# A hybrid scan and Fourier layer: read-out and state copies moved to ScalarE, branch products spread, one division of PSUM

## The chip, the cores and the metric

The kernel runs on one core of a Trainium2 chip. The core has TensorE (PE: matmuls, with their weight loads as PEld), VectorE (DVE), ScalarE (ACT), GpSimd (POOL) and SyncE (SP, which here issues nearly all DMAs). Each engine works through its own queue in order; semaphores make one wait for another. The metric is the device time of one execution in microseconds, given as the median of several runs.

## The reference, cut to what matters

One layer of a diffusion backbone for 128 context and 1024 latent tokens (T = 1152 in all), width 1024:

```python
proj = h @ w_in                       # q, ff, fb, v, zA, u, zB, gA, gB
# branch A: gated linear recurrence, forward and backward, 8 heads, dk = dv = 128
S_t = diag(f_t) S_{t-1} + k_t v_t^T ;  o_t = S_t^T q_t
o = (o_f + o_b) * rsqrt(mean(o*o) + EPS) * gnorm_w
yA = o * silu(zA)
# branch B: real part of a 2-D DFT over positions and channels of u
yB = yF * silu(zB)
merged = sigmoid(gA) * (yA @ w_pa) + sigmoid(gB) * (yB @ w_pb)
out = merged @ w_o                    # then residual and final norm
```

The final states of the context tokens (both directions, every head) are an output as well (`new_state`).

## The kernel before, in words

All float32 products are made as three float32r products of a high and a low part (`mm3`: high by high, high by low, low by high). So each weight block is loaded, its high part is cast on ACT (`w_hi`, `wh`), and the low part is subtracted on POOL or DVE (`w_lo`, `wl`).

The stages in order of time are: normalisation and the first gate (to about 100 us); v for all heads (`project_v`, to about 164 us); the other columns of `w_in`, in pairs of 128 columns by a seven-product scheme (`pair`, to about 850 us, with the Fourier branch and the first scan levels interleaved); the scans with the branch products in between (about 850 to 1163 us); the last branch products and `w_o` to the end.

PSUM has eight banks. Up to the end of v they are divided into `d` (six banks, used in turn by the first gate and v) and `s` (two). Then that division is closed and another one is opened: `d` two, `s` two, `o` four. The pairs take `d`, `o`, `o` in turn (`any_ps`). A tile of the new division waits until the tile of the old one that lay on its bank has been read.

The scans are run by a loop over n = 0 to 9 (here: rounds). Round n walks a string of letters, `PATTERN[n]`, and each letter advances one generator by one step:

- **E** (`scan_blocks`, head n): five steps, E1 to E5, for the block sizes 4, 8, 16 (lines 781 to 792), 32 and 64. Each runs small matmuls over km, kk and qq into an `s` bank, and grows kk and qq by decay factors on DVE (L465, in place, 128x1152). The merges into a32 (L479) are on DVE, the copies into km (L472) and att (L803 to L816) on ACT.
- **L** (`scan_rest`, head n-1): transposes of kk (kt_ps, copied by ACT, L843), then the products kv and the state chain S on DVE (L856), then three groups of read-out matmuls into `o` banks. In the chain the first chunk of each direction gives the new state: `ns`, copied out of PSUM on DVE (L853) and stored by SP (L861). After each read-out group ACT squares and sums (L885) and takes the root (L887), and DVE takes the reciprocal (L869) and multiplies (L870, `scaled`).
- **Y** (the rest of `scan_rest`, head n-2): transpose of the scaled read-out, multiplication by the gate gz on DVE (L899), store to DRAM by SP (L908).
- **F** (`dense`): one half of a branch product. 12 matmuls go into a `d` bank, and DVE multiplies by the gate and so evacuates it: L936, or L938 followed by an add on POOL (L939). Each F loads its gate tile (gs) on SP, with three buffers; every second F loads a new weight block.
- **V** (`late_v`): the part of v that is left for here.

The order of matmuls on PE in the scans is that of the letters, forced by dependencies (`queued`). The order on the other engines is set by the scheduler's own timeline of the program. `ns` has no buffer of its own: it takes turns with the gz tiles in a ring of three (tag `gz`), and a gz slot is free when its store has landed.

Of the kernel before, what the change touches and what calls it, by code (L numbers as in the profile page):

```python
# [11 lines left out]
F32 = mybir.dt.float32  # L12
F32R = mybir.dt.float32r
I32 = mybir.dt.int32
AF = mybir.ActivationFunctionType
ALU = mybir.AluOpType
PSUM = bass.MemoryType.PSUM

P = 128
# [6 lines left out]
TW = 384  # L26
# [26 lines left out]
LATE = (4, 8, 16)  # L53
GRAN = 4
PIECES = ((0, 640), (640, T))
PATTERN = (['VEVVEVVEVVEVVE', 'VEVLVLEVVLVELVVLEVLFELFLF'] + 6 * ['EYLFYLEYLFELFFFEFLELFLF'] +
           ['YLFYLFYLFLFFFLFLFLF', 'YFYFYFFF'])
HW = T // 2
W0 = 1280
# [11 lines left out]
def diffusion_step(ctx: ExitStack, tc: tile.TileContext, xT, x_tok, w_pr, w_v, w_ada, w_ada_gt,  # L71
                   w_pab, w_o, state, vecs, b_gt, fnorm, pos_c, pos_row_t, pos_col_t, masks_i, mask_d, chan_dft, ctx_dft,
                   seq_dft, sign_row, y, new_state):
    nc = tc.nc

    def pool(name, bufs, **kw):
        return tc.tile_pool(name=name, bufs=bufs, reuse_waits="tile", **kw)
# [3 lines left out]
    banks = {}  # L81

    def open_psum(**bufs):
        stack = ExitStack()
        for tag, n in bufs.items():
            banks[tag] = stack.enter_context(pool("ps_" + tag, n, space=PSUM))
        return stack

    psum = open_psum(d=6, s=2)

    v_dr = dram.tile([NH, P, NCH, P], F32, name="v_dr")
    ya_dr = dram.tile([NH, P, T], F32, name="ya_dr")
# [19 lines left out]
        yield  # L112
        tc.cur_priority = p + 1

    def dense_ps():
        return banks["d"].tile([P, 512], F32, tag="d", name="d_ps")

    def scan_ps(tag="s"):
        return banks[tag].tile([P, 512], F32, tag=tag, name=tag + "_ps")

    ident = const.tile([P, P], F32, name="ident")
    make_identity(nc, ident)
# [92 lines left out]
    with pool("st", 1, side="right") as st, pool("st2", 2, side="right") as st2:  # L215
# [119 lines left out]
        e_ps = {}  # L335

        def gate0(k, a, b):

            for i in range(2):
                w_ = slice(i * P, (i + 1) * P)  # L340
                if k == 0:
                    e_ps[i, a] = dense_ps()[:, :b - a]
                ps = e_ps[i, a]
                mm3(ps, [(e_hi[:, k, w_], e_lo[:, k, w_], *h_at(k, a, b))], nc.tensor.matmul, k == 0, k == KT - 1)
                if k == KT - 1:
                    n = -(-(b - a) // SW)
                    w = (b - a) // n
                    for p in range(n):
                        go = va.tile([P, SW], F32, tag="vo", name="go", bufs=2)[:, :w]
                        nc.scalar.activation(go, ps[:, p * w:(p + 1) * w], AF.Sigmoid)  # L350
                        nc.sync.dma_start(g_dr[i, 0, :, a + p * w:a + (p + 1) * w], go)


        warm = dense_ps()
        e_raw = vb.tile([P, KT, 2 * P], F32, tag="wr", name="w_raw")
        e_hi, e_lo = (va.tile([P, KT, 2 * P], F32R, tag="w" + x, name="e_" + x) for x in "hl")
        was, abs_ = [], []
# [41 lines left out]
    def project_v(pr, chunks, p):  # L399
        raw = vb.tile([P, KT, 2 * P], F32, tag="wr", name="w_raw")  # L400
        nc.sync.dma_start(raw, w_v[pr])
        hi, lo = split_w(raw, KT, 2 * P, p)
        for c in chunks:
            ps = dense_ps()[:, :2 * P]
            mm3(ps, [(*h_at(k, c * P, (c + 1) * P), hi[:, k, :], lo[:, k, :]) for k in range(KT)])
            vo = va.tile([P, SW], F32, tag="vo", name="vo", bufs=2)[:, :2 * P].rearrange("p (h v) -> p h v", h=2)
            nc.vector.tensor_copy(vo, ps)
            nc.sync.dma_start(v_dr[2 * pr:2 * pr + 2, :, c, :].rearrange("h p v -> p h v"), vo)
# [8 lines left out]
    with pool("tg", 1, side="right") as tg:  # L417
        for nth, pr in enumerate((0, 2, 1, 3)):
            with tc.issue_after(last_ada[-1].ins):
                project_v(pr, range(5 if pr in LATE_V else 0, NCH), (vb, va)[nth % 2])  # L420
            for k in ((0,1,2,3), (), (), ())[pr]:
                for j in range(2):
                    js = slice(j * SW, (j + 1) * SW)
                    r = tg.tile([P, 2, 2, SW], F32, name="r")
                    for d in range(2):
                        for t, x in enumerate((h1, h2)):
                            hi, lo = x[k + 4 * d]
                            nc.gpsimd.tensor_tensor(out=r[:, d, t, :], in0=hi[:, js].bitcast(F32), in1=lo[:, js].bitcast(F32),
                                                    op=ALU.add)
# [5 lines left out]
                        nc.scalar.copy(hi[:, js], ts[:, w])  # L435
                        nc.vector.tensor_tensor(out=lo[:, js], in0=ts[:, w], in1=hi[:, js].bitcast(F32), op=ALU.subtract)
    ph1.close()
    psum.close()
    psum = open_psum(d=2, s=2, o=4)
    banks_in_turn = cycle("doo")  # L440

    def any_ps():
        return scan_ps(next(banks_in_turn))
# [380 lines left out]
    def scan_rest(hd):  # L824
        kk, qq, att, tot = heads.pop(hd)
        vt = s1.tile([P, T], F32, name="vt").rearrange("p (c v) -> p c v", v=P)
        nc.sync.dma_start(vt, v_dr[hd])
        S = s1.tile([P, 2, KT, P], F32, name="S")
        nc.sync.dma_start(S[:, 0, 0, :], state[0, hd])
        nc.sync.dma_start(S[:, 1, KT - 1, :], state[1, hd])  # L830


        ns = s2.tile([P, TW], F32, tag="gz", name="ns", bufs=3)[:, :2 * P].rearrange("p (d v) -> p d v", d=2)
        jobs = [(0, 0), (1, 0)]
        for j in range(KT - 1):
            jobs += [(0, 1 + j), (1, KT - j)]
        kts = []
        for b in range(0, len(jobs), 4):
            kt_ps = scan_ps("o")
            for n, (d, c) in enumerate(jobs[b:b + 4]):  # L840
                transpose(kt_ps[:, n * P:(n + 1) * P], in_=kk[:, d, c * P:(c + 1) * P], identity=ident)
            kts.append(s2.tile([P, HW], F32, name="kt_sb", bufs=4)[:, :4 * P].rearrange("p (c t) -> p c t", c=4))
            nc.scalar.copy(kts[-1], kt_ps)  # L843
            if b % 8:
                yield
        for b in range(0, len(jobs), 4):
            kv = scan_ps("o")
            for n, (d, c) in enumerate(jobs[b:b + 4]):
                matmul(kv[:, n * P:(n + 1) * P], lhsT=kts[b // 4][:, n, :], rhs=vt[:, c, :], start=True, stop=True)
            for n, (d, c) in enumerate(jobs[b:b + 4]):  # L850
                kvn = kv[:, n * P:(n + 1) * P]
                if c == 0:
                    nc.vector.tensor_copy(ns[:, d, :], kvn)  # L853
                else:
                    j = c - 1
                    nc.vector.scalar_tensor_tensor(out=S[:, d, j + (-1 if d else 1), :], in0=S[:, d, j, :],  # L856
                                                   scalar=tot[:, d, c:c + 1], in1=kvn, op0=ALU.mult, op1=ALU.add)
            if b % 8:
                yield
        for d in range(2):  # L860
            nc.sync.dma_start(new_state[hd, d], ns[:, d, :])  # L861


        ss = s1.tile([P, NCH], F32, name="ss", bufs=2)
        ons = []

        def scaled(g, ps, on):
            sg = ss[:, 3 * g:3 * g + 3]
            nc.vector.reciprocal(sg, sg)  # L869
            nc.vector.tensor_tensor(out=on, in0=ps[:, :TW].rearrange("p (c v) -> p c v", v=P),  # L870
                                    in1=sg.unsqueeze(2).broadcast_to([P, 3, P]), op=ALU.mult)
            ons.append(on)

        for g in range(3):
            ps = scan_ps("o")
            for c in range(3 * g, 3 * g + 3):
                oc = ps[:, (c - 3 * g) * P:(c - 3 * g + 1) * P]
                matmul(oc, lhsT=att[:, c, :], rhs=vt[:, c, :], start=True, stop=c == 0)
                if c:
                    for d in range(2):  # L880
                        matmul(oc, lhsT=qq[:, 1 - d, c * P:(c + 1) * P], rhs=S[:, d, c - 1, :], start=False, stop=d == 1)

            on = s2.tile([P, HW], F32, tag="kt_sb", name="on", bufs=4)[:, :TW].rearrange("p (c t) -> p c t", c=3)
            for c in range(3):
                nc.scalar.activation(on[:, c], ps[:, c * P:(c + 1) * P], AF.Square, accum_out=ss[:, 3 * g + c:3 * g + c + 1])  # L885
            sg = ss[:, 3 * g:3 * g + 3]
            nc.scalar.activation(sg, sg, AF.Sqrt, bias=eps, scale=1.0 / P)  # L887
            if g:
                scaled(g - 1, *last)
            last = ps, on  # L890
            yield
        scaled(2, *last)
        for g in range(3):
            gz = s2.tile([P, TW], F32, name="gz", bufs=3)
            nc.sync.dma_start(gz, gz_dr[hd, :, g * TW:(g + 1) * TW])
            yt = scan_ps("o")
            for c in range(3):
                transpose(yt[:, c * P:(c + 1) * P], in_=ons[g][:, c, :], identity=ident)
            nc.vector.tensor_tensor(out=gz, in0=yt[:, :TW], in1=gz, op=ALU.mult)  # L899
            if hd == NH - 1 and g < 2:  # L900

                if g == 0:
                    ys2.append(new_y(3, 0))
                a, b = g * TW, min((g + 1) * TW, HW)
                hi, lo = (x[:, a:b] for x in ys2[3])
                nc.scalar.copy(hi, gz[:, :b - a])
                nc.vector.tensor_tensor(out=lo, in0=gz[:, :b - a], in1=hi.bitcast(F32), op=ALU.subtract)
            nc.sync.dma_start(ya_dr[hd, :, g * TW:(g + 1) * TW], gz)  # L908
            yield
# [92 lines left out]
    for n in range(NH + 2):  # L1002
# [3 lines left out]
        done, rest = rest, scan_rest(n - 1) if 0 < n <= NH else iter(())  # L1006
        for what in PATTERN[n]:
            next({"E": blocks, "L": rest, "Y": done, "F": fill, "V": late}[what], None)
# [8 lines left out]
    op = ctx.enter_context(pool("op", 1))  # L1017
# [46 lines left out]
    for c in range(NCH):  # L1064
# [3 lines left out]
        for ks in [slice(k, k + 1) for k in range(KT)] if c == 0 else [slice(0, KT)]:  # L1068
            nc.scalar.copy(mh[:, ks, :], merged[:, ks, cs_])
            (nc.gpsimd if c else nc.vector).tensor_tensor(out=ml[:, ks, :], in0=merged[:, ks, cs_],  # L1070
                                                          in1=mh[:, ks, :].bitcast(F32), op=ALU.subtract)
# [17 lines left out]
        for n, (a, b) in enumerate(((0, 512), (512, 768), (768, D)) if last else ((0, 512), (512, D))):  # L1089
            ns_ = slice(a, b)  # L1090
            ps = any_ps()[:, :b - a]
# [115 lines left out]
```

## Time and profile before

| | before |
|---|---|
| median of 3 runs | 1323.48 us (1321.5 to 1328.47) |
| the profiled execution | 1325.72 us, span 1323.9 us |
| busy: PE / PEld | 1246.3 us (94%) / 1172.0 us (89%) |
| busy: DVE / ACT / POOL | 843.2 (64%) / 624.4 (47%) / 475.3 us (36%) |
| mean granted TensorE clock | 0.981 |

How to read the rows that follow: a row of the timeline has start and length in microseconds, engine, source line, operation, output <- input, shapes and count; in brackets stand the idle time of the engine before it and what ended that. A row of a view by windows has the stretch, its length, and for each engine its busy time in it. A row of waits has total, number and longest. PEclk is the granted TensorE clock (1.00 is full).

### The profile page before, as it was taken

Reading aid. Unit: us, or ns where it says so; the run is one execution under the profiler, and the core shown is the slowest. Engines: PE = TensorE matmul, PEld = TensorE weight load, DVE = VectorE, ACT = ScalarE, POOL = GpSimd, SP = SyncE. Lnnn points to the kernel's source line nnn. Section 1 sums busy time; section 2 is a strip of 40 time slices with the busy share of each in tenths; the row PEclk is TensorE's granted clock in tenths of the full one; section 3 lists DMA queues with packets and bytes.
Section 4 is the critical chain, followed back from the end, with each engine's and each line's share of the span. In section 5 each row is a group of like instructions: output and inputs, shape, how many; then the busy total and the mean of one; then the engine's idle time right before and its main releaser. Section 6 shows DMA issues by size and latency. Waiting matters only on the chain. (4 is left out here: it accounts for less than half of the span.)

```text
span 1323.9 us, 31278 instructions
## 1 busy us (share of the span) xinstructions
PE 1246.3 (94%) x12768; PEld 1172.0 (89%) x12768; DVE 843.2 (64%) x1391; ACT 624.4 (47%) x1290; POOL 475.3 (36%) x359
## 2 busy tenths in 40 slices
PE   4899999999999999999999999987988989999998
PEld 2679999999989999999999998987888879999886
DVE  7737743434357677677767645486878988475554
ACT  5542232454446655655655544454544545332332
POOL 4515523233412312222121216432232445565563
PEclk8899989999999999999999999998999999999999
DMA  8542233434444655555555663765666754676432
GB/s 313 220 172 60 76 109 118 135 101 148 146 153 163 209 179 165 201 184 161 204 186 163 213 227 106 251 229 165 225 210 220 241 176 131 186 241 198 141 121 96
DMA packets 126162, 229.88 MB, mean 174 GB/s; under 512 B 11441, under 2 KB 78786, under 8 KB 121794
## 3 DMA queue, kind: packets, MB, share of 16 engines
q1 hardware_dynamic: 125730, 226.83, 51.6%
q8 instruction: 100, 1.64, 0.5%
q10 hardware_dynamic: 288, 1.05, 0.3%
q14 instruction: 44, 0.36, 0.1%
HBM read 154.82 MB, written 73.02 MB: 172 GB/s over the span
## 5 line engine op out<-in xcount | busy, mean ns | idle before, releaser
L628 POOL TENSOR_TENSOR wl<-raw,wh 128x512 fp32r<-128x512 f32 x81 | 114.7, 1416 | 449.6 <-ACT wh L627 448.1
L627 ACT CAST wh<-sa 128x512 fp32r<-128x512 f32 x81 | 50.3, 621 | 130.3 <-DVE sa L645 58.4
L187 POOL TENSOR_TENSOR w_lo<-w_raw,w_hi 128x512 fp32r<-128x512 f32 (+1 forms) x36 | 65.4, 1817 | 125.4 <-ACT w_hi L185 125.3
L628 DVE TENSOR_TENSOR wl<-sa,wh 128x512 fp32r<-128x512 f32 x81 | 60.2, 743 | 73.9 <-ACT wh L627 73.5
L627 ACT CAST wh<-raw 128x512 fp32r<-128x512 f32 x108 | 66.3, 614 | 78.5 <-DMA raw<-in_w_pr 40.2
L201 PE MATMUL o_ps<-h1h,wh 128*128 128x288 f32 x324 | 98.8, 305 | 0.0
L201 PE MATMUL d_ps<-yh,w_hi 128*128 128x288 f32 x256 | 82.3, 321 | 16.4 <-DVE merged L936 8.2
L201 PE MATMUL o_ps<-h1l,wh 128*128 128x288 f32 x324 | 96.5, 298 | 0.0
L201 PE MATMUL o_ps<-h1h,wl 128*128 128x288 f32 x324 | 96.5, 298 | 0.0
L645 DVE TENSOR_TENSOR sa<-raw 128x512 f32<-128x512 f32 x27 | 31.0, 1149 | 85.0 <-DMA raw<-in_w_pr 85.0
L939 POOL TENSOR_TENSOR merged<-merged,gs 128x288 f32<-128x288 f32 x64 | 61.1, 968 | 58.5 <-DVE gs L938 58.0
L201 PE MATMUL d_ps<-yh,w_lo 128*128 128x288 f32 x256 | 78.1, 305 | 4.0 <-POOL w_lo L187 4.0
L201 PE MATMUL d_ps<-yl,w_hi 128*128 128x288 f32 x256 | 77.4, 302 | 0.0
L465 DVE TENSOR_TENSOR kk<-kk,fa 128x1152 f32<-128x1152 f32 x40 | 59.7, 1493 | 15.4 <-PE s_ps L201 7.9
L465 DVE TENSOR_TENSOR qq<-qq,fa 128x1152 f32<-128x1152 f32 x40 | 67.6, 1691 | 1.6 <-PE s_ps L201 1.4
L201 PEld LDWEIGHTS d_ps<-yh,w_hi 128*128 128x128 f32 x256 | 49.9, 195 | 18.5 <-DVE merged L936 9.1
L665 DVE TENSOR_TENSOR c<-o_ps,x 128x288 f32<-128x288 f32 x108 | 47.2, 451 | 26.2 <-PE o_ps L201 19.8
L201 PEld LDWEIGHTS o_ps<-h1h,wh 128*128 128x128 f32 x324 | 61.4, 189 | 1.0 <-issue 0.3
L201 PEld LDWEIGHTS o_ps<-h1h,wl 128*128 128x128 f32 x324 | 61.3, 189 | 0.6 <-issue 0.6
L201 PEld LDWEIGHTS o_ps<-h1l,wh 128*128 128x128 f32 x324 | 61.5, 190 | 0.1
L655 ACT COPY x<-d_ps 128x288 f32<-128x288 f32 x81 | 32.1, 396 | 61.0 <-PE d_ps L201 60.9
L201 PEld LDWEIGHTS d_ps<-yh,w_lo 128*128 128x128 f32 x256 | 50.0, 195 | 4.9 <-POOL w_lo L187 4.9
(389 smaller groups left out, 4609.6 us busy)
## 6 DMA issues: line engine op xcount, KB each, us to landing
raw<-in_w_pr SPq DMA_DIRECT2D x52, 512.0 KB, 4.7
gs<-g_dr SPq DMA_DIRECT2D x96, 144.0 KB, 3.2
w_raw<-in_w_pab SPq DMA_DIRECT2D x44, 256.0 KB, 2.8
f_dr<-c SPq DMA_DIRECT2D x32, 288.0 KB, 3.2
kk<-kk_dr SPq DMA_DIRECT2D x8, 1152.0 KB, 7.1
qq<-qq_dr SPq DMA_DIRECT2D x8, 1152.0 KB
wa<-in_w_ada SPq DMA_DIRECT2D x8, 1024.0 KB
g_dr<-c SPq DMA_DIRECT2D x28, 288.0 KB, 3.4
```

The source lines that it names most:

```text
L187: eng.tensor_tensor(out=lo, in0=raw, in1=hi.bitcast(F32), op=ALU.subtract)
L201: queued(nc.tensor.matmul(*args, **kw))
L465: nc.vector.tensor_tensor(out=xv, in0=xv, in1=view(ff, off, [[2 * mg, n], [step, 2], [0, m]]), op=ALU.mult)
L627: nc.scalar.copy(hi, src)
L628: eng.tensor_tensor(out=lo, in0=src, in1=hi.bitcast(F32), op=ALU.subtract)
L645: nc.vector.tensor_tensor(out=out, in0=x, in1=y, op=op)
L655: nc.scalar.copy(x[i, j], ps["a", j])
L665: nc.vector.tensor_tensor(out=c[:, h], in0=ps[bank, j], in1=x[i, j], op=ALU.add)
L939: nc.gpsimd.tensor_tensor(out=out, in0=out, in1=gs, op=ALU.add)
```

## The change

Four edits. The product by the reciprocal root in `scaled` goes from one DVE instruction per group to three on ACT, each with its scale from a column. The copy into `ns` goes from DVE to ACT. In rounds 2 to 7 one F is taken out of the run of three and put ahead of the Y between E2 and E3. PSUM is divided once, at the start, as it was divided from the pairs on; the first gate and v take their banks from `o` and `d` in the order o d o d o o.

```diff
-PATTERN = ([..., ...] + 6 * ['EYLFYLEYLFELFFFEFLELFLF'] +
+PATTERN = ([..., ...] + 6 * ['EYLFYLEFYLFELFFEFLELFLF'] +
...
-    psum = open_psum(d=6, s=2)
+    psum = open_psum(d=2, s=2, o=4)
+    first_banks = cycle("ododoo")
...
-                    e_ps[i, a] = dense_ps()[:, :b - a]
+                    e_ps[i, a] = scan_ps(next(first_banks))[:, :b - a]
...
-        warm = dense_ps()
+        warm = scan_ps(next(first_banks))
...
-            ps = dense_ps()[:, :2 * P]
+            ps = scan_ps(next(first_banks))[:, :2 * P]
...
     ph1.close()
-    psum.close()
-    psum = open_psum(d=2, s=2, o=4)
     banks_in_turn = cycle("doo")
...
                 if c == 0:
-                    nc.vector.tensor_copy(ns[:, d, :], kvn)
+                    nc.scalar.copy(ns[:, d, :], kvn)
...
             nc.vector.reciprocal(sg, sg)
-            nc.vector.tensor_tensor(out=on, in0=ps[:, :TW].rearrange("p (c v) -> p c v", v=P),
-                                    in1=sg.unsqueeze(2).broadcast_to([P, 3, P]), op=ALU.mult)
+            for c in range(3):
+                nc.scalar.activation(on[:, c], ps[:, c * P:(c + 1) * P], AF.Identity, scale=sg[:, c:c + 1])
```

More of the change, by code (lines that the diff above doesn't have):

```diff
@@ L55 @@
 PIECES = ((0, 640), (640, T))
-PATTERN = (['VEVVEVVEVVEVVE', 'VEVLVLEVVLVELVVLEVLFELFLF'] + 6 * ['EYLFYLEYLFELFFFEFLELFLF'] +
+PATTERN = (['VEVVEVVEVVEVVE', 'VEVLVLEVVLVELVVLEVLFELFLF'] + 6 * ['EYLFYLEFYLFELFFEFLELFLF'] +
            ['YLFYLFYLFLFFFLFLFLF', 'YFYFYFFF'])
@@ L113, in later, with dense_ps @@
         tc.cur_priority = p + 1
-    def dense_ps():
-        return banks["d"].tile([P, 512], F32, tag="d", name="d_ps")
     def scan_ps(tag="s"):
         return banks[tag].tile([P, 512], F32, tag=tag, name=tag + "_ps")
+    def dense_ps():
+        return scan_ps("d")
     ident = const.tile([P, P], F32, name="ident")
```

## The prediction

> **What bounds the kernel now.** I read the page's busy times first, then the stretches by windows, then TensorE's (PE's) waits in the scans, then the timelines around the longest ones.
>
> ```profile
> PE 1246.3 (94%) x12768; PEld 1172.0 (89%) x12768; DVE 843.2 (64%) x1391; ACT 624.4 (47%) x1290; POOL 475.3 (36%) x359
> PE   4899999999999999999999999987988989999998
> PEclk8899989999999999999999999998999999999999
> ```
>
> PE is the bound nearly everywhere; what is missing is in the startup, one slice near 170 us, and the scans (about 845 to 1160 us). In the scans each round n of the last loop runs five E steps (E1 to E5) of one head, among L, Y and F steps of others. The next view cuts rounds 2 to 7 from the end of E1's matmuls to the start of E5's.
>
> ```profile
> core 0: us, PE busy (x) PEld busy (x) DVE busy (x) ACT busy (x) POOL busy (x), PEclk, DMA share, GB/s
> 923.90:949.04 25.14, 21.84 (x356) 20.66 (x357) 22.75 (x42) 11.79 (x20) 7.91 (x5) 0.93 0.79 260
> 958.47:984.48 26.01, 22.09 (x361) 20.97 (x360) 22.00 (x40) 12.58 (x26) 8.02 (x5) 0.93 0.79 260
> 1060.85:1090.00 29.15, 22.88 (x360) 21.12 (x360) 24.26 (x42) 11.43 (x24) 12.01 (x11) 0.94 0.61 186
> 1099.42:1120.97 21.55, 20.64 (x359) 19.64 (x360) 20.78 (x39) 11.34 (x25) 12.93 (x9) 1.00 0.56 164
> sum 149.93, PE 129.24 PEld 121.65 DVE 133.25 ACT 70.45 POOL 56.87; mean PE 21.54 PEld 20.27 DVE 22.21 ACT 11.74 POOL 9.48
> 949.04:957.64 8.60, 8.60 (x96) 8.38 (x96) 5.11 (x13) 5.58 (x26) 1.27 (x1) 1.00 0.37 99
> ```
>
> The last row is the other part of a round, E5 to the next E1: PE is busy for all of its 8.60 us and nothing but fewer matmuls would shorten it. The first part is different: the same 360 matmuls take 21.55 us in round 7 and 29.15 in round 6, and DVE (VectorE) is busy longer than PE (133.25 against 129.24 us in the six). So DVE's queue sets this part, and PE's waits there say how:
>
> ```profile
> PE d_ps L201 <- DVE merged L936: 8.2, 4, 2.6
> PE d_ps L201 <- DVE gs L938: 5.0, 2, 3.5
> PE d_ps L201 <- POOL w_lo L187: 4.0, 4, 1.9
> PE s_ps L201 <- DVE qq L465: 3.7, 5, 1.3
> PE o_ps L201 <- DVE S L856: 3.3, 1, 3.3
> ```
>
> The first two rows are F steps that found neither of the two "d" banks free. Round 3 shows the chain:
>
> ```profile
> 965.18 0.54 DVE L899 TENSOR_TENSOR gz<-o_ps,gz 128x384 f32<-128x384 f32 x1
> 967.53 0.49 DVE L853 COPY ns<-o_ps 128x128 f32<-128x128 f32 x2 [1.81 <-DMA ya_dr<-gz]
> 974.61 0.29 DVE L468 TENSOR_TENSOR fa<-fa 128x72 f32<-128x72 f32 x1
> 975.32 0.82 DVE L936 TENSOR_TENSOR merged<-gs,d_ps 128x288 f32<-128x288 f32 x2
> 972.89 0.29 PE L201 MATMUL d_ps<-yh,w_lo 128*128 128x288 f32 x1
> 975.83 0.40 PE L201 MATMUL d_ps<-yh,w_hi 128*128 128x288 f32 x1 [2.64 <-DVE merged L936]
> 976.93 0.44 PE L201 MATMUL d_ps<-yh,w_lo 128*128 128x288 f32 x1
> 957.64 0.83 PE L201 MATMUL s_ps<-qq,km 128*32 128x32 f32 x72
> 987.95 1.59 PE d_ps L201 x12
> 1120.97 1.23 PE L201 MATMUL s_ps<-qq,kk 128*64 128x64 f32 x35 [0.80 <-DVE qq L465]
> DVE ns L853 <- DMA ya_dr<-gz: 5.6, 4, 2.7
> ```
>
> The third F in a row waits 2.64 us for a bank whose evacuation (merged) stands on DVE behind everything that was held up when the copy into ns waited 1.81 us for its slot (ns shares a ring of three buffers with gz, and a store of gz was still under way). Rounds 3 to 6 each have such a stall, 5.6 us in all, and round 7 has none: its third F did not wait. After such a gap the clock is halved for a while: the same matmul took 0.29 us before and 0.44 after, and the granted clock of this round's part is 0.93.
>
> **The change part by part.**
>
> *The F that moves (rounds 2 to 7).* "E L F F F E" becomes "E L F F E", and the third F goes ahead of the Y L F between E2 and E3. All F come from one generator, so the second to the fourth F come one place earlier. What moves with one: 12 matmuls (1.59 us in the chain's row), one evacuation on DVE (L936 or L938), for the second input also one add on POOL (L939), one gs load on SP's queue, and for every second F a weight load on SP, its cast on ACT and its subtraction on POOL. On PE it passes one Y and the L with the first two kv groups, which come 1.6 us later; so do E3 and the S updates on DVE. On SP the load passes the store of gz that ns waits for. Instead of the third F, E4 stands where PE waited, and E4 needs no "d" bank; the F after it comes later by a step like E1's 0.83 us. The weights of the sixth F can be cast one F earlier, as their slot is freed by the third; that bears on the w_lo row.
>
> *New states copied on ACT.* Sixteen copies leave DVE, a pair per head at 0.49 us (row above), and with them the 5.6 us of stalls. ACT takes them and the waits. An ACT read of the same shape is the Square below at 275 ns: 16 x 0.275 = 4.4 us on ACT. If its cover goes, what stands behind on ACT is the next head's km copy and att, which waits for DVE itself.
>
> *Read-out scaled on ACT.* Twenty-four multiplies of 553 ns (13.3 us) leave DVE; 72 ACT instructions of 128x128 come. The reciprocal stays on DVE. No row has a scale from a column at this shape, so it is bounded: below by the Square, above by adding what two column operands cost in the forget gate, 863 - 682 = 181 ns.
>
> ```profile
> L870 DVE TENSOR_TENSOR on<-o_ps,ss 128x384 f32<-128x384 f32 x24 | 13.3, 553 | 0.5
> L885 ACT ACTIVATE on<-o_ps 128x128 f32<-128x128 f32 x72 | 19.1, 275 | 32.7 <-PE o_ps L201 32.6
> L712 ACT ACTIVATE c<-c,lb,omlb 128x576 f32<-128x576 f32 x32 | 27.1, 863 | 0.5
> L711 ACT ACTIVATE c<-c 128x576 f32<-128x576 f32 x32 | 21.8, 682 | 3.4 <-DVE c L665 2.3 <-DMA gz_dr<-c 0.8
> ```
>
> Bounds 275 and 456 ns; I take one operand, 365: 72 x 0.365 = 26.3 us on ACT (20 to 33), 1.1 per group against DVE's 0.55. Two of a head's three groups fall into the 8.60 us part: ACT's 5.58 us become 7.8, still under 8.60, and its idle time before L885 (32.6 us, waiting for PE) is the cover. DVE's relief here is mostly in that part, where PE is the bound, so it counts as nothing. If the cover goes, the km copy and a w_hi cast come up to 1.1 us later.
>
> The Trainium skill speaks against this move: in "ScalarE: Activation LUTs", Rules for kernel authors, a mul belongs on VectorE and not on ScalarE. Its section What ACT_TABLE_LOAD costs gives 186 ns + 0.833 ns per element and 93 for a pointer operand, an estimate of 386 ns here and 27.8 us for the 72, in place of 26.3; the sum below stays the same by it as long as the cover holds. No row of this trace has such an instruction; for one without a pointer the page gives 293 and the Square's row 275.
>
> *Sum for rounds 2 to 7.* DVE's work in the six parts is 133.25 us; without six pairs of ns copies (2.9) it is 130.3. Round 7, with neither DMA stall nor third-F wait, took 21.55 - 20.78 = 0.77 us more than DVE's work; I give each part the same 0.77 (4.6 in all): 134.9 instead of 149.93, a gain of 15.0. PE's own work, 6 x 20.64 = 123.8 at round 7's full clock, is less and does not bind. The spells of slower clock lie inside the lengths of now. Bounds: at best DVE's 130.3 (gain 19.6), at worst 147.0 (rival 1).
>
> *One division of PSUM.* Six banks in the order o d o d o o are the same ring of six as before, so startup and v do not change. What goes is the seam:
>
> ```profile
> 164.19:174.04 9.85, 5.59 (x24) 5.62 (x24) 6.84 (x10) 3.19 (x6) 2.54 (x2) 0.65 0.35 120
> 165.41 0.62 ACT L627 CAST wh<-raw 128x512 fp32r<-128x512 f32 x1 [4.42 <-DMA raw<-in_w_pr]
> 166.16 1.26 POOL L628 TENSOR_TENSOR wl<-raw,wh 128x512 fp32r<-128x512 f32 x1 [7.40 <-ACT wh L627]
> 167.89 0.41 DVE L407 COPY vo<-d_ps 128x256 f32<-128x256 f32 x1
> 168.45 0.58 PE L201 MATMUL d_ps<-h1h,wh 128*128 128x288 f32 x1 [4.26 <-DVE vo L407]
> 169.06 0.44 PE L201 MATMUL d_ps<-h1h,wl 128*128 128x288 f32 x1
> ```
>
> The first pair's bank lies on that of one of the last v tiles, whose copy stands on DVE until 167.89. In the ring the pair begins on a bank whose tile is five back, free long before. Next late are the weights: wh at 166.03, wl at 167.42, so the third matmul can go at about 167.45 instead of 169.06: 1.6 us. PE still idles some 3 us, so I leave the halved clock (0.65 over 9.85 us, 3.4 us lost) as it is; range 0 to 5.0.
>
> *Round 1.* No F moves. One pair of ns copies leaves the S chain (PE waited 3.3 us for it): 0.4 us.
>
> Total: 15.0 + 1.6 + 0.4 = 17.0 us. The profiled execution took 1325.7 us (span 1323.9), so 1308.7; the median of the runs is 2.2 lower, which would make 1306.5. I take 1308.
>
> **The rivals.** 1) *The wait only changes its place.* DVE stays dense between E1 and E5, E5's wait for qq (3.7 us above) grows by what the F wait loses, and S, now 1.6 us later for the moved F, takes the place of the DMA stall. Then only the ns work (2.9) and the seam's 1.6 are won: 1323.5 - 4.5 = 1319.0. For it: round 7 without any stall still waits 0.80 us at E5. Against: round 7 is 4.5 us shorter than round 3 with the same work.
>
> 2) *Slower: ns holds SP's queue.* The store of ns (L861) is issued by SP in order, ahead of gs and gz loads. If the copy stands on ACT behind att L803, it ends some 6.7 us later than now in round 3:
>
> ```profile
> 972.98 1.75 ACT L803 COPY att<-fa 32x288 f32<-32x288 f32 x4 [3.45 <-DVE fa L479]
> 967.85 0.82 SPq L861 DMA_DIRECT2D out_state<-ns  x2
> 972.94 0.42 SPq L931 DMA_DIRECT2D gs<-g_dr  x1
> gs<-g_dr SPq DMA_DIRECT2D x96, 144.0 KB, 3.2
> ```
>
> (974.73 against 968.02.) The gs load of 972.94 would then go after 974.7 and land 3.2 us later, with three buffers hiding about two F (3.2 us): 3 us lost a round and a halved clock (1.7): 6 x 4.7 = 28, less the 17: 1323.5 + 11 = 1334.5. It decides once ns ends more than 3 us after E3. Against: ACT was idle 3.45 us before that att.
>
> 3) *The read-out lands on the path.* The ScalarE rule of the Trainium skill quoted above points this way. From rows: 1.1 - 0.55 us on each of 24 groups is 13 us lost of the 17: 1323.5 - 4 = 1319.5. It needs the transposes of "on" to wait; ACT's idle time before L885 speaks against it.
>
> **How the numbers follow.** Forecast 0.60 (1300 to 1316); the full bounds, gain 19.6 + 5.0 + 0.4, 1298.5, 0.05; rival 1 0.20; rival 2 0.10; rival 3 0.05. From 1299 to 1322 leaves out rival 2 and little else. About 0.5% (6.6 us, below 1316.9 or above 1330.1) is what a measurement can tell from no change. Faster: 0.60 + 0.05 and a quarter of rivals 1 and 3 (0.06), 0.71; slower: rival 2 less its milder half, 0.07; same 0.22.
>
> **What would show it.** The six parts from E1 to E5 near 22.5 us, DVE idle before ns gone and ACT idle in its place; no PE gap over 2 us between E3 and E5 and fewer halved-clock spells there; at the seam PE released by wl. Wrong if E5's wait for qq grows beyond 2 us a round, if SP's gs loads land later than their F, or if DVE's order puts merged behind still more.

## The result, and the profile after

The changed kernel took 1308.26 us (median of four runs, 1305.2 to 1312.09) beside 1324.22 us for the kernel before on the same chip: ratio 0.9883 [0.9856, 0.9909], 16 us faster. The forecast was 1308 us, in a range of 1299 to 1322. The total was right; the step on the new states was not, the length of the six parts came out shorter than forecast, and what the read-out is worth stays unsettled.

The profiled execution took 1312.09 us (span 1310.2), the slowest of the four, against 1325.72 (span 1323.9) of before. So the two traces explain 13.6 of the 16 us. First the busy times of the whole execution, PE's busy tenths and the granted clock, from the page of after:

```profile
PE 1249.0 (95%) x12768; PEld 1174.9 (90%) x12768; DVE 830.3 (63%) x1351; ACT 647.3 (49%) x1378; POOL 470.9 (36%) x359
PE   5999989999999999999999999988999989999997
PEclk8799999999999999999999999998999999999999
```

DVE lost 12.9 us of work and ACT gained 22.9, while PE's sum hardly moved. The change shows in rounds 2 to 7. The same view by windows as before, from the end of E1's matmuls to the start of E5's:

```profile
core 0: us, PE busy (x) PEld busy (x) DVE busy (x) ACT busy (x) POOL busy (x), PEclk, DMA share, GB/s
927.08:947.90 20.82, 20.18 (x357) 19.36 (x357) 19.59 (x36) 12.72 (x26) 7.08 (x5) 1.00 0.92 304
957.34:979.49 22.15, 20.48 (x360) 19.70 (x360) 21.90 (x37) 13.16 (x29) 8.02 (x5) 1.00 0.90 300
988.91:1009.76 20.85, 20.43 (x359) 19.64 (x360) 20.62 (x37) 12.07 (x25) 6.43 (x4) 1.00 0.85 285
1051.06:1075.31 24.25, 20.81 (x360) 19.60 (x360) 22.49 (x39) 14.21 (x39) 13.49 (x10) 1.00 0.72 229
sum 130.04, PE 122.74 PEld 117.59 DVE 126.06 ACT 74.73 POOL 54.83; mean PE 20.46 PEld 19.60 DVE 21.01 ACT 12.46 POOL 9.14
```

The six parts fell from 149.93 to 130.04 us, and the clock is full in all of them. They are now 4 us longer than DVE's work, where before they were 16.7 us longer. PE's waits in the scans (rounds 2 to 7) say what is left:

```profile
PE s_ps L202 <- DVE qq L464: 5.6, 6, 1.8
PE s_ps L202 <- ACT att L804: 1.4, 1, 1.4
PE o_ps L205 <- ACT kt_sb L842: 1.0, 1, 1.0
PE d_ps L202 <- DVE gs L937: 0.6, 1, 0.6
```

The wait for merged (8.2 us) is gone and that for gs is down from 5.0 to 0.6 us. The wait of E5 for qq is still there, once a round, and has grown (before had 3.5 us in four of these rounds). New are a wait for att and one for the copy kt_sb, once each. Round 3 as it now stands on DVE and ACT:

```profile
965.31 0.43 ACT L852 COPY ns<-o_ps 128x128 f32<-128x128 f32 x2 [0.31 <-PE o_ps L202]
971.33 1.76 ACT L802 COPY att<-fa 32x288 f32<-32x288 f32 x4 [1.57 <-DVE fa L478]
973.70 0.43 DVE L935 TENSOR_TENSOR merged<-gs,d_ps 128x288 f32<-128x288 f32 x1
974.07 0.59 DVE L855 SCALAR_TENSOR_TENSOR S<-S,tot,o_ps 128x128 f32<-128x128 f32 x2
974.59 0.43 DVE L935 TENSOR_TENSOR merged<-gs,d_ps 128x288 f32<-128x288 f32 x1
976.79 2.55 DVE L464 TENSOR_TENSOR qq<-qq,fa 128x1152 f32<-128x1152 f32 x1
```

The copy of ns waits only 0.31 us, for the matmul that feeds it, and DVE runs without a break up to the qq of E5, where PE waits 1.7 us. The part between E5 and the next E1, 8.60 us before, is unchanged but for one round:

```profile
947.90:956.60 8.70, 8.70 (x105) 8.47 (x109) 4.11 (x10) 6.60 (x31) 1.27 (x1) 1.00 0.48 136
1040.03:1050.23 10.20, 8.80 (x96) 8.43 (x96) 6.67 (x9) 7.77 (x29) 8.73 (x7) 1.00 0.34 101
```

(The first row reaches 0.1 us into the next E1.) Round 5 has the wait of 1.4 us for att. From E1 of round 2 to E5 of round 7 the two traces differ by 18.3 us (197.90 to 179.61). Outside it after is 4.6 us longer: 1.2 up to the end of v, 0.5 from there to the first scan, 1.4 in rounds 0 and 1, 1.4 in the end.

### The profile page after: what moved, and what is told of

The parts are those of the page before. It is cut to its first block, busy times and chain, and to the rows that moved or that the text cites. A ratio compares the mean times of both kernels' runs of the same rounds, so it can differ in the third digit from the quotient of the medians.

```text
span 1310.2 us, 31299 instructions
## 1 busy us (share of the span) xinstructions
PE 1249.0 (95%) x12768; PEld 1174.9 (90%) x12768; DVE 830.3 (63%) x1351; ACT 647.3 (49%) x1378; POOL 470.9 (36%) x359
## 5 line engine op out<-in xcount | busy, mean ns | idle before, releaser
L464 DVE TENSOR_TENSOR qq<-qq,fa 128x1152 f32<-128x1152 f32 x40 | 64.8, 1621 | 3.5 <-PE s_ps L202 3.1
L464 DVE TENSOR_TENSOR kk<-kk,fa 128x1152 f32<-128x1152 f32 x40 | 56.6, 1414 | 13.8 <-PE s_ps L202 5.7
L186 ACT CAST w_hi<-w_raw 128x512 fp32r<-128x512 f32 (+1 forms) x48 | 35.0, 729 | 34.3 <-issue 12.5
```

The costliest lines, as they stand in the source:

```text
L186: nc.scalar.copy(hi, raw)
L464: nc.vector.tensor_tensor(out=xv, in0=xv, in1=view(ff, off, [[2 * mg, n], [step, 2], [0, m]]), op=ALU.mult)
```

## The experiments

Two theories stood against each other. *One cause*: the three F in a row are the stall, the new order is the change, and the two moves to ACT and the division of PSUM add little. *Joint cause*: the order only removes waits, DVE's queue still has to be shortened to collect the gain. Each experiment is timed against the kernel before on the same chip (whose medians lie between 1324.10 and 1325.62 us), so the ratios are what to compare; lengths inside the execution come from one trace each. "Scan" is the time from the start of E1 in round 2 to the start of E5 in round 7 in its own trace, "work" is DVE's busy time in the six parts.

| kernel | median us | ratio to before | scan | six parts | work |
|---|---|---|---|---|---|
| before | | | 197.90 | 149.93 | 133.25 |
| order alone | 1317.83 | 0.9958 [0.9935, 0.9981] | 194.54 | 138.30 | 133.70 |
| ns on ACT alone | 1324.10 | 1.0004 [0.9980, 1.0028] | 194.35 | 146.37 | 130.36 |
| read-out on ACT alone | 1323.44 | 0.9996 [0.9975, 1.0016] | 193.92 | 145.95 | 132.61 |
| PSUM alone | 1323.32 | 1.0004 [0.9978, 1.0031] | 197.71 | 149.73 | 134.50 |
| all but the order | 1321.68 | 0.9974 [0.9954, 0.9994] | 192.54 | 144.57 | 128.88 |
| all but ns | 1316.42 | 0.9930 [0.9910, 0.9950] | 184.04 | 131.13 | 130.02 |
| all but the read-out | 1314.46 | 0.9919 [0.9892, 0.9947] | 183.25 | 130.29 | 127.65 |
| all but PSUM | 1309.40 | 0.9876 [0.9843, 0.9908] | 180.96 | 130.55 | 129.10 |
| after | 1308.26 | 0.9883 [0.9856, 0.9909] | 179.61 | 130.04 | 126.06 |

### One part alone

```diff
-    6 * ['EYLFYLEYLFELFFFEFLELFLF']     # only the order
+    6 * ['EYLFYLEFYLFELFFEFLELFLF']
```

> The kernel before with the new order of letters alone (the third F moved in rounds 2 to 7). Theory Q (DVE's queue: the gain comes where a late item on DVE holds a bank that PE wants, so order and stalls count): the third-F waits (11.6 us in six rounds) go, but the ns copy still stalls DVE for its slot, so the six parts from E1 to E5 come down from 149.9 us to about 143, and the time falls by 4 to 8 us. Rival W (DVE's amount of work alone sets these parts; the order of F changes nothing): the parts stay within 2 us of 149.9 and the time within 2 us of before.

The order takes away most of the waiting by itself: the six parts are 4.6 us longer than DVE's work (138.30 - 133.70), as forecast for after (0.77 each). That is less than the 143 us of theory Q, which kept the stall of ns: in this trace ns, still on DVE, does not wait for its slot at all. But the work stays at 133.70, and part of the gain is given back between E5 and E1, in rounds 3 and 5. By windows, from the start of E5 to the end of E1, for rounds 2, 3 and 5:

```profile
951.02:960.46 9.44, 9.44 (x169) 9.17 (x170) 5.95 (x14) 5.15 (x24) 1.27 (x1) 1.00 0.44 135
983.97:996.18 12.21, 12.21 (x169) 11.89 (x170) 5.89 (x14) 4.76 (x20) 1.27 (x1) 0.75 0.35 103
1049.25:1064.16 14.91, 12.20 (x169) 11.74 (x170) 8.22 (x14) 9.58 (x35) 11.16 (x8) 0.77 0.43 127
```

The same 169 matmuls took 9.44 us at full clock and 12.21 at 0.75. In the six rounds E5 now waits 9.4 us for qq, against 3.5 in four rounds before. PE's waits ahead of and in the two long ones were these:

```profile
PE s_ps L201 <- DVE qq L465: 2.9, 1, 2.9
PE s_ps L201 <- ACT att L805: 2.7, 1, 2.7
```

So the order alone gained 11.6 us in the six parts and lost 8.3 of them behind E5. That leaves 3.4 us of the scan in this trace, whose execution was the slowest of the twelve (1323.79 us); the total of all twelve fell by 0.42% or 5.6 us, and 3.4 us lies within its interval.

```diff
-                    nc.vector.tensor_copy(ns[:, d, :], kvn)      # only the new states
+                    nc.scalar.copy(ns[:, d, :], kvn)
```

> The kernel before with the copies into ns on ACT alone. Theory Q: DVE loses the stalls (5.6 us in rounds 3 to 6) and 2.9 us of copies; the third F, now without a stall behind it, waits under 1 us as in round 7; the six parts fall from 149.9 to 138 to 142 and the time by 8 to 11 us. Rival W: only the 2.9 us of work count, parts 147, time lower by 3 us. Rival S (ACT's late copy holds the store queue): time higher than before.

No gain in time, so theory Q failed; the six parts came to what rival W forecast (147), the total did not. Its waits on ACT and DVE show why:

```profile
ACT ns L853 <- DMA ya_dr<-gz: 6.1, 4, 3.1
DVE S L856 <- ACT ns L853: 4.5, 5, 2.4
```

The copy still waits for its slot, now on ACT, and DVE's update of S, which reads the same PSUM tile, waits for the copy. The stall of 5.6 us didn't leave DVE; it came back by another name. The Trainium skill ("PSUM — Partial Sum Buffer", PSUM bank collisions raise a hardware error) says that the compiler's scheduler orders any two instructions on different engines that touch the same bank in the same quadrant, reads among them. The 4.5 us of S behind ns agree with that. In the trace with the order alone, ns has no such wait although it is on DVE and its buffer is shared as before: its matmuls come 1.6 us later, when the slot is free.

```diff
-            nc.vector.tensor_tensor(out=on, in0=ps..., in1=sg..., op=ALU.mult)   # only the read-out
+            for c in range(3):
+                nc.scalar.activation(on[:, c], ps[:, c * P:(c + 1) * P], AF.Identity, scale=sg[:, c:c + 1])
```

> The kernel before with the read-out scaled on ACT alone. Theory Q: DVE's relief lies mostly in the part E5 to E1, where PE is busy throughout, so the time changes by 0 to -2 us, the six parts stay at 148 to 150. Rival W: 13.3 us of work leave DVE, about a tenth of its load in a round, and the time falls by 5 us or more. Rival A (the read-out comes onto the path on ACT): the part E5 to E1 grows from 8.60 us, time higher by 2 us or more.

Nothing either way in the total: the 13.3 us that leave DVE gain nothing while the third F still waits (merged 6.2, gs 3.7 us). The six parts were shorter than theory Q had them (145.95 us, not 148 to 150). Here and with ns on ACT alone the scan of the one trace is 3.6 to 4.0 us shorter than before's, which the totals of twelve executions each do not show; why, stays open.

```diff
-    psum = open_psum(d=6, s=2)          # only PSUM: first_banks, no second division
+    psum = open_psum(d=2, s=2, o=4)
+    first_banks = cycle("ododoo")
```

> The kernel before with one division of PSUM alone. Theory Q: only the seam between v and the pairs gains, 1.2 to 1.6 us for the bank and up to 3.4 us where a halved-clock spell is shortened; the six parts of the scans stay at 150; time lower by 1 to 3 us, hardly to be told from no change. Rival P (the division moves more than the seam, since the scheduler orders DVE and ACT anew after it): the scans' parts change by over 3 us either way.

Nothing. At the seam its PE waits for wh and then for wl, as forecast:

```profile
PE d_ps L202 <- ACT wh L626: 2.0, 1, 2.0
PE d_ps L202 <- POOL wl L627: 0.9, 1, 0.9
```

### All but one

```diff
-    6 * ['EYLFYLEFYLFELFFEFLELFLF']     # the changed kernel with the old order
+    6 * ['EYLFYLEYLFELFFFEFLELFLF']
```

> The kernel after with the old order of letters (three F in a row). Alone the new order gained 5.5 us and the two moves to ACT nothing. Theory Q2 (the three Fs in a row are the place where anything late on DVE reaches PE; without them taken apart the relief on DVE is lost again in the third F's wait): 1320 to 1324, six parts at 143 to 147 us. Rival W2 (relief on DVE adds up to a gain once both moves are made together): 1313 to 1316, parts at 138 or less.

Without the order the other three give 0.26% [0.06, 0.46]. DVE's work is down to 128.88 us and the six parts are still 15.7 us longer than it; S waits 4.0 us for ns, ns 5.6 us for its slot. This is the reverse of the order alone: less work, the waits kept, as Q2 forecast. The order alone gave 0.42%, the other three without it 0.26%, all four 1.17%. That is 0.49% more than the sum; the three intervals, added in squares, make about 0.4%. So the joint cause is borne out, by a narrow margin.

```diff
-                    nc.scalar.copy(ns[:, d, :], kvn)             # the changed kernel, ns on DVE
+                    nc.vector.tensor_copy(ns[:, d, :], kvn)
```

> The kernel after with the copy into ns back on DVE. Q2 (with the Fs apart, the stall of the copy for its slot and 2.9 us of copies are what still holds DVE): 1312 to 1315, six parts about 136 to 139 us with stalls of DVE before ns of 4 us or more in all. Rival R (the read-out is what made the combination): 1308 to 1310, parts at 131 to 133.

> The kernel after with the read-out scaled on DVE again. Q2: the read-out lies in the part where PE is busy throughout, so 1307 to 1310, six parts within 3 us of 130. Rival R (the read-out is what made the combination): 1314 or more, parts at 136 or more, or the part E5 to E1 over 8.6 us in several rounds as in the run with the order alone.

The second of these is the changed kernel with the read-out's product back on DVE. Both have six parts near 131 us, within 1.1 us of after, but both lose 3.4 us between E5 and E1: the five stretches sum to 47.93 and 47.98 us against 44.59. The stall of 4 us or more that Q2 gave the first one isn't there: ns, on DVE and in the shared ring, never waits for its slot. Q2's times were missed in both (1316.42 and 1314.46 us, above its ranges); the second came out as its rival R forecast, by the long stretches behind E5. Round 5 of the kernel with ns on DVE, from the start of E5 to the end of E1, and PE's wait in it:

```profile
1038.86:1053.22 14.36, 11.24 (x169) 10.82 (x170) 7.30 (x11) 11.93 (x44) 11.17 (x9) 0.88 0.45 120
```

```profile
PE s_ps L202 <- ACT att L804: 3.1, 1, 3.1
```

```diff
-        ns = s2.tile([P, TW], F32, tag="gz", name="ns", bufs=3)[...]   # ns on DVE, buffer of its own
+        ns = s1.tile([P, 2 * P], F32, name="ns")...
```

> The kernel after with the copy into ns back on DVE and ns in a buffer of its own, so that it never waits for a store of gz. Q2: the stall is gone but the 2.9 us of copies are back on DVE: 1309 to 1312, six parts 132 to 135 us. If the stall is all that counts, the same as after (1308); if the amount of work is, the same as the run with the copy back on DVE in the shared ring.

A buffer of its own for ns, with the copy on DVE and the rest changed, gave 0.9955 [0.9938, 0.9971], no better than the shared ring (0.9930 [0.9910, 0.9950]); 1309 to 1312 us had been forecast, 1318.95 came. Its work is 133.06 us and round 5 again has the wait for att (3.40 us). The slot of ns is therefore not what is left to gain once the order has changed. DVE's work is 3 us higher than with the shared ring; 2.9 of them lie in round 2, which ran at a granted clock of 0.93 and took 24.54 us against 21.05. Whether the buffer or a single execution's chance did that, one trace doesn't settle.

### The wait for att

All kernels with the new order and the casts of ya on ACT wait in round 5 for att, which frees an s bank for E5. ACT's timeline in the changed kernel shows what stands ahead of it:

```profile
1037.31 0.68 ACT L921 CAST yh<-yr 128x576 fp32r<-128x576 f32 x1 [0.98 <-DMA yr<-ya_dr]
1037.89 0.61 ACT L186 CAST w_hi<-w_raw 128x512 fp32r<-128x512 f32 x1
1040.01 0.67 ACT L921 CAST yh<-yr 128x576 fp32r<-128x576 f32 x1 [1.51 <-DMA yr<-ya_dr]
1040.59 1.59 ACT L804 COPY att<-s_ps 32x288 f32<-32x288 f32 x4
```

The casts of the next input (ya) wait on ACT for their loads, and att stands behind them in the queue. The next three kernels move these four casts to POOL.

```diff
-        nc.scalar.copy(hi, yr)
+        (nc.gpsimd.tensor_copy if cast_pool else nc.scalar.copy)(hi, yr)   # cast_pool: first half of ya
```

> Changed kernel, with the four casts into yh for the first half of input ya taken from ACT to POOL (GpSimd); nothing is left out. Theory: in round 5 these casts wait for their loads (yh waits 7.2 us for yr in 22 us) and hold the copies of E4 into att behind them, which E5 waits for. Then the wait of s_ps for att (1.40 us) goes, E5 to E1 of round 5 falls from 10.20 to 8.60 us, and the kernel gains 1.6 us plus what round 6 (24.25 us against 21 in the others) loses to the same block, up to 3 us: ratio to before 0.985 to 0.987. Rival: each cast and subtraction then stand one after the other on POOL (about 2.8 us a tile against 1.6), the yr slots come free later and the first F of ya waits for POOL: 3 to 5 us lost, ratio 0.990 to 0.992.

> The same move of the four casts, with the new states copied on DVE as before (the order of letters, the read-out on ACT and the one division of PSUM stay). With the casts on ACT this kernel stood at 0.993 [0.991, 0.995] and its E5 to E1 in round 5 took 13.53 us, att waited for 3.12 us. Theory: the difference to the changed kernel (0.9883) is this block in round 5 and not DVE's work: round 5's stretch falls to 8.6 us, 5 us gained, ratio 0.988 to 0.990. Rival: copies of ns on DVE cost by themselves, wherever the casts stand: ratio 0.992 or more.

> The same move of the four casts, with the read-out scaled on DVE as before (order, ns on ACT, PSUM division stay). With the casts on ACT it stood at 0.9919 [0.9892, 0.9947] and E5 to E1 took 10.00 and 12.17 us in rounds 4 and 5. Theory: again the block behind the casts: 8.6 us in both, 4 to 5 us gained, ratio 0.987 to 0.989, that is, the read-out's engine costs nothing. Rival: the read-out on DVE costs by itself: ratio 0.991 or more.

The wait for att went, as forecast, and the gain did not come. It is gone from all three, and the ratios are 0.9894 [0.9863, 0.9924], 0.9912 [0.9882, 0.9942] and 0.9925 [0.9893, 0.9957], beside 0.9883, 0.9930 and 0.9919 with the casts on ACT: no difference outside the intervals. The theory's ratio was missed in all three; the third came out as its rival forecast. In the first of them round 5, which had waited 0.45 us for qq and 1.40 for att, now waits 2.05 us for qq, and in round 3 the wait for qq grew from 1.67 to 2.10:

```profile
PE s_ps L202 <- DVE qq L464: 2.1, 1, 2.1
```

From the start of E5 to the end of E1 rounds 3 and 5 then took

```profile
973.72:984.70 10.98, 10.98 (x169) 10.66 (x170) 5.41 (x11) 6.95 (x29) 2.39 (x2) 0.84 0.47 139
1039.01:1049.95 10.94, 10.94 (x169) 10.62 (x170) 7.15 (x11) 9.14 (x37) 8.58 (x7) 0.84 0.35 95
```

In the second, PE waited for the casts on their new engine, 3.9 us in two waits:

```profile
PE d_ps L202 <- POOL yh L921: 2.8, 1, 2.8
PE d_ps L202 <- POOL yl L922: 1.1, 1, 1.1
```

The block on ACT was real but not what separates these kernels: E5 has DVE's qq to wait for as well (in the third kernel 2.19 and 2.04 us in rounds 4 and 5, where att had been waited for). With the casts on POOL the two kernels that keep ns or the read-out on DVE still stand above after, but the intervals overlap. What each of the two moves is worth in the presence of the order, 2 to 6 us by the ratios, is not settled better than that.

> Kernel before with the order of letters, the copies of ns and the read-out on ACT, but the two divisions of PSUM as before; nothing is left out. Alone the one division was worth 0 (1.0004 [0.9978, 1.0031]). Theory: so it is here, 0 to 1.6 us: ratio 0.988 to 0.990. Rival: with the new order the six shared banks in the scans matter, or the seam's 1.2 us and the spell of slower clock come through: 3 us or more, ratio 0.991 or more.

That is the kernel before with the order, ns and the read-out changed and the two divisions of PSUM kept: 0.9876 [0.9843, 0.9908], the same as after. PE waits at the seam as before (vo, 4.5 us) and it costs nothing that the total shows. No version tried beats the changed kernel outside the intervals.

## Why the prediction came out right, step by step

**The bound (right).** The rule "length of a part = DVE's work + about 0.8 us where nothing stalls" held for kernels that it was not made from: 4.6 us over the work with the order alone, 4.0 in after, 2.6 without the read-out, 1.1 without ns. Kernels with the old order stand 13.3 to 16.7 us over it.

**The sum for rounds 2 to 7 (right in kind, mis-sized).** Forecast 134.9 us, measured 130.04, which is under even the bound of 130.3 given as the best; the term that was off is DVE's work, 130.3 in the sum and 126.06 in the trace. Only the 2.9 us of ns copies were taken off it. By instruction, in the same windows, kk's growths took 32.5 us instead of 35.3, the evacuations, six fewer, 15.1 instead of 16.1, the updates of S 24.4 instead of 25.1, and 0.6 us of products went as well (sums over single instructions, which overlap a little, so they add up to more than the difference). The excess of 0.77 us a part, taken from one round, was 0.66.

The term for kk shows why DVE's work could not be carried over as a fixed amount. Of the 160 growths of kk and qq in the two traces, all 78 that ran beside no POOL instruction took 1.33 to 1.36 us, and all 41 that took over 1.5 us, up to 2.59, ran beside one; the other 41 ran beside one too and lost little or nothing. Two growths and a subtraction of round 3 of after:

```profile
965.22 1.33 DVE L464 TENSOR_TENSOR kk<-kk,fa 128x1152 f32<-128x1152 f32 x1
968.56 2.34 DVE L464 TENSOR_TENSOR qq<-qq,fa 128x1152 f32<-128x1152 f32 x1
968.41 1.27 POOL L188 TENSOR_TENSOR w_lo<-w_raw,w_hi 128x512 fp32r<-128x512 f32 x1 [5.87 <-ACT w_hi L186]
```

What the growths of kk in the six parts took above 1.35 us each fell from 4.3 to 1.5 us, which is the whole of their change; that of qq went from 8.0 to 8.5. No run moved POOL's work to test this.

**New states on ACT (wrong as a mechanism).** The step "DVE loses the copies, and with them the 5.6 us of stalls" failed. The copy alone gained nothing, since S on DVE waited for ns on ACT (4.5 us). It is the moved F that removed the stall: with the new order and ns on DVE (the order alone, and all but ns) the copy never waits for its slot. The term was booked once, so the sum didn't suffer; only its owner was wrong.

**Read-out on ACT (price right, worth not settled).** The estimate of 365 ns for each instruction met the group's row in after:

```profile
L870 ACT ACTIVATE on<-o_ps,ss x72: 359/370/414, 907.4 to 1142.9; 128x128 f32<-128x128 f32 x72
```

The Trainium skill ("ScalarE: Activation LUTs", What ACT_TABLE_LOAD costs) makes it an estimate of 386 ns; the measured median of 370 lies between that and the forecast's 365. ACT's cover held but for one place: `on` waited for DVE's reciprocal, 3.8 us in all, and PE never for `on`; in round 6 the last products (0.89 us) and the km copy stood on ACT ahead of the copy kt_sb, for which PE waited 0.98 us. But "DVE's relief counts as nothing" isn't borne out for certain. With the product back on DVE the scan of its one trace was 3.6 us longer (183.25 against 179.61), by the waits behind E5. Alone the move was worth nothing in the total; with the order the ratios differ by 0.36%, within their intervals, so its worth stays open. The rule in the same page's Rules for kernel authors, which puts a mul on VectorE, spoke against the move; with VectorE's queue as the bound the kernel with the move was not slower than the one without (0.9883 [0.9856, 0.9909] against 0.9919 [0.9892, 0.9947], intervals that just overlap).

**The seam (mechanism right, gain not seen).** PE was released by wh and wl, as said: 2.24 and 0.87 us of waits in place of 4.26, and the third matmul follows v's end by 3.65 us instead of 4.87.

```profile
167.67 0.40 PE L202 MATMUL d_ps<-h1h,wh 128*128 128x288 f32 x1 [2.24 <-ACT wh L626]
169.07 0.40 PE L202 MATMUL d_ps<-h1h,wl 128*128 128x288 f32 x1 [0.87 <-POOL wl L627]
```

That is 1.2 us for a forecast of 1.6. It doesn't reach the total: the first scan begins at 853.2 us on average over the nine traces with one division and at 852.8 over the five with two, each spread over 849 to 855.5. The spread is larger than the term, so a term of this size could not be tested by totals at all.

**Round 1 (the wait as forecast).** PE's wait for S there went from 3.3 to 2.8 us, 0.5 for a forecast of 0.4. The stretch as a whole did not get shorter (below).

**The rivals.** Rival 1, the wait that only changes its place, came true in part: with the order alone the wait at E5 grew from 3.5 to 9.4 us and much of the gain was lost there. That the 5.6 us left lie near the rival's price of 4.5 is chance, since that price was made of the ns copies and the seam. With the moves to ACT the wait grew to 5.6 us and stayed under the 2 us a round named as the sign of failure (longest 1.83). Rival 2 needed ns to end late; it ended at 965.7 us, 5.6 us ahead of att, and its store went out at once:

```profile
965.77 1.25 SPq L860 DMA_DIRECT2D out_state<-ns  x2
970.97 0.42 SPq L930 DMA_DIRECT2D gs<-g_dr  x1
```

Rival 3 needed the transposes to wait for `on`, and they did not; the 0.98 us for kt_sb in round 6 are the nearest to it on PE.

**Where the total was lucky.** The scans gained 18.3 us in the traces (19.9 in the six parts, less 1.6 behind E5 of round 5) for a forecast of 15.0; the seam and what lies outside gave nothing, and those stretches were 4.6 us longer in this execution. The two errors have opposite signs. Where rounds 0 and 1 took 1.4 us longer the granted clock was lower. The first row is before, the second after:

```profile
852.67:923.07 70.40, 59.29 (x1014) 56.10 (x1014) 51.58 (x72) 31.72 (x69) 20.55 (x11) 0.93 0.61 213
```

```profile
854.43:926.25 71.82, 62.12 (x1013) 58.56 (x1013) 50.11 (x71) 34.13 (x79) 17.74 (x11) 0.88 0.60 208
```

Whether the change brings these spells or a single execution has them by chance stays open; the medians of several runs, 16 us apart, speak for some chance in it.

## What to carry to other kernels

When one engine's queue sets a stage, write the stage's length as that engine's work plus its waits, and price an edit by which of the two it moves: here the order took 12 us of waits and left the work, the moves to ACT took 4 to 8 us of work and left the waits, and alone the order gave 5.6 us and each of the others nothing, together 16. Do not take the engine's work for a fixed amount: here growths beside POOL took up to 2.59 us instead of 1.35. A stalled instruction that is moved to an idle engine can bring its stall back if another engine works in the same tile, as S did behind ns. And before you repair a new wait, ask what the waiting engine would wait for next: moving the casts from in front of att gained nothing, since qq then came as late (2.05 us of waits in round 5 where qq and att had made 1.85).

## What the runs showed of the hardware

The clock's fall after a gap isn't a matter of the gap's length alone. At E5, waits for qq of up to 1.83 us left the clock at 1.00 in after; in the first kernel with the casts on POOL 2.1 us took it to 0.84 and cost 1.5 us on the same 169 matmuls, and with the order alone 2.9 us took it to 0.75 and cost 2.8. But at the same place, E5 of round 3, the second kernel with the casts on POOL waited 2.23 us, and the clock stayed full:

```profile
978.69:988.11 9.42, 9.42 (x169) 9.15 (x169) 5.41 (x11) 6.93 (x29) 2.39 (x2) 1.00 0.54 157
```

By windows of after, the stretch from E5 in round 6, which follows a wait of 1.83 us, and one among the pairs with a single idle time of 1.82 us:

```profile
1075.31:1084.73 9.42, 9.42 (x169) 9.15 (x170) 4.56 (x11) 6.93 (x29) 2.95 (x4) 1.00 0.30 89
549.00:562.00 13.00, 11.18 (x137) 10.58 (x136) 10.55 (x18) 8.19 (x16) 1.81 (x2) 0.87 0.41 139
```

And in before, a stretch with a single idle time of 2.72 us:

```profile
387.00:400.00 13.00, 10.28 (x114) 10.04 (x113) 9.31 (x12) 6.40 (x10) 1.27 (x1) 1.00 0.44 159
```

So a gap of 1.8 us was followed by a slower clock in one place and by a full one in the other, one of 2.1 us by a slower clock, and gaps of 2.23 and 2.72 us by a full one. The Trainium skill ("TensorE: Matmul & The Clock Gate", What's actually happening) has the clock decided by a window of about 3.4 us that runs freely, so that the moment of a gap counts beside its length. These rows agree with that. They do not agree with a reading of the same page's advice (Why this matters for your kernels: no gaps over about 3 us) by which shorter gaps are safe.
